# Second product of all six gathered tiles on TensorE, four tokens wide, with a ring of nine shared buffers

## The chip, the cores and the metric

The kernel runs on one core of a Trainium2 chip. The metric is the device time of one launch in microseconds (us), lower is better. TensorE (PE) multiplies, VectorE (DVE) and ScalarE (ACT) work on tiles, GpSimd (POOL) issues the indirect DMAs that gather rows, and SyncE (SP) issues most other DMAs. Each engine takes its instructions in the order in which the program has them.

## The reference

One encoder layer of width 1024 is applied to two groups of tokens, a prompt of 256 and a sample of 1024. Two mixers (a gated recurrence and an attention with low-rank projections) are merged and added to the input. Then a mixture of 16384 small experts follows, and a last norm:

```python
def block(zt):                      # 128 tokens, after the norm with norm_ffn
    ...                             # per token and head (8) the 16 best experts: ids eidx, softmax weights g
    u = jnp.take(u_tab, eidx, axis=0)
    ve = jnp.take(v_tab, eidx, axis=0)
    act = jax.nn.gelu(jnp.einsum('td,thkd->thk', zt, u).astype(jnp.float32), approximate=False) * g
    return jnp.einsum('thk,thkd->td', act.astype(zt.dtype), ve)
...
x = x + _peer(_rmsnorm(x, norm_ffn[l]), ...)
return _rmsnorm(x, norm_final)
```

Each token picks 8 x 16 = 128 experts, so that a tile of 128 tokens needs 128 x 128 rows of 4 KB from each of the two tables. All values are float32.

## The kernel before

Tokens are handled in ten tiles of 128. The experts of six tiles are gathered: the prompt's two (`rP`), the sample's first two (`r0`) and its last two (`r1`). The four tiles between (`rd`) take every expert, with weight zero where it was not picked (`dense`): there TensorE streams both tables, split exactly into two float32r parts, in 2 x 3 x 1024 products of 512 columns.

For a gathered tile `u_steps` makes the first product. For each of its 128 slots one indirect DMA (L933) brings the rows of `peer_u` for all tokens into a buffer `ug`, and one DVE instruction (L935) multiplies them with the normed tokens and sums. Then comes the GELU. The second product has two forms:

- `v_steps` (tiles `rP` and the first of `r0`) works token by token on TensorE. One indirect DMA (L963) brings the 128 picked rows of one token into a buffer `vg`, with picks on the partitions. The token's activations stand in one column of a 32-column block of zeros (`zt`), and a product with it adds the token's result to its row of the PSUM tile `acc` (L970). Tokens of different blocks of 32 use different column groups of the array (`tile_position=(0, g_ * 32)`). Two tokens (VG = 2) are taken together: half row of the first, half row of the second, then the other halves. A float32 product shows as two MATMUL records.
- `v_slots` (the second tile of `r0` and both of `r1`) works slot by slot on DVE: one gather (L989), one multiply-add into the tile `vacc` (L991).

`ug`, `vg` and some scratch share a ring of five buffers of 128 x 1024 float32. The norm vectors `gfin` and `gffn` are loaded once and stay. `experts` takes a step of a tile's first product and a step of the previous tile's second product in turn; the steps of the second product are given high priority.

The order on each engine is written by a planner (`schedule_with_timeline_sim=True`) which runs the program on its own timing model, and puts an instruction in place when its inputs are there in the model; among those that are, high priority goes first. On the chip this order is fixed: PE waits at an instruction whose rows have not landed. `experts(rP)` and `experts(r0 + r1)` are two calls, so a tile's second product runs beside the first product of the next tile of the same call. The last call and `dense` come at the end of the program, and run beside each other.

Of the kernel before, what the change touches and what calls it, by code (L numbers as in the profile page):

```python
# [12 lines left out]
F32 = mybir.dt.float32  # L13
# [11 lines left out]
P = 128  # L25
# [13 lines left out]
VG = 2  # L39
# blocks of the input projection, 128 columns each  # L40
B_Q, B_FF, B_FB, B_I, B_G, B_CQ, B_CKV, B_GLH, B_GLA, B_PE = 0, 4, 8, 12, 16, 20, 23, 25, 33, 41
# columns of the gains
# [8 lines left out]
def encoder(ctx, tc, I, O, dbg=None):  # L51
# [10 lines left out]
    # ---------------------------------------------------------------- constants  # L62
# [21 lines left out]
    # lower bounds: softmax over the two rows, first row  # L84
# [33 lines left out]
    # ---------------------------------------------------------------- helpers  # L118
# [8 lines left out]
    # Operands of the large products come either whole, as (x,) in float32, or split exactly in two  # L127
    # float32r parts, as (high, low).
# [25 lines left out]
    def put(dst, src):  # L154
        # dst: the parts of src
        if len(dst) == 1:
            nc.scalar.copy(dst[0], src)
        else:
            nc.scalar.copy(dst[0], src)  # L159
            nc.vector.tensor_tensor(dst[1], src, dst[0].bitcast(F32), op=OP.subtract)  # L160

    def rsqrt_to(pool, out, src, inv_n, shape, name, vy=None):
        # (src * inv_n + EPS) ** -0.5, one Newton step on exp(-ln/2)
# [9 lines left out]
    def rsqrt_small(pool, out, src, inv_n, shape, name):  # L173
        # the same on VectorE alone, for a few elements: three Newton steps from the exponent's half
# [11 lines left out]
    def norm_T(pool, xs, nk, n, name, bank, fold=False):  # L186
        # xs: [128, n] each, features on partitions; rsqrt of the mean square, on all partitions
# [15 lines left out]
    # ---------------------------------------------------------------- input projection  # L203
    def project(s0, S, ap, wpool, bank, np_, whole):
        """Norm, then blocks of the projection into DRAM; a generator, so that users of the blocks
        can be put between them."""
# [83 lines left out]
    # ---------------------------------------------------------------- HGRN2, one head  # L290
# [3 lines left out]
    def prefixes(hp, f, n, dirs, tg, nb):  # L294
        """From forget gates [P, len(dirs), n] (0 backward, 1 forward): inputs' gates in place of f, prefixes of
        the logarithms inside chunks (backward exclusive, forward inclusive), and the chunks' totals."""
# [26 lines left out]
    def xexp(hp, fb, tot, di, t0, comp, tag):  # L323
        # exp of the prefix, or of what is left to the chunk's end
# [12 lines left out]
    def hgrn_states(s0, S, h, dirs, hp, nb, bank):  # L337
        """States at the chunks' starts."""
# [42 lines left out]
    def hgrn_out(s0, S, h, t0, hp, nb, bank, pre=None):  # L381
        """Outputs of LS tokens: scores inside chunks, level by level, and the states' share."""
# [83 lines left out]
    # ---------------------------------------------------------------- attention  # L466
# [11 lines left out]
    def attn_prep(s0, S, bp, wpool, bank, va, spill):  # L478
        """Latents' norms, then values, and per head keys and queries; these two go to DRAM when spill is set."""
# [8 lines left out]
        for dst, b0, nk, gc in ((ck, 0, 2, G_KVA), (cq, 3, 3, G_QA)):  # L488
# [6 lines left out]
            else:  # L495
                # read into the low part, and split there
# [5 lines left out]
        # keys' rotary part, shared by the heads  # L502
# [13 lines left out]
        # values, token on partitions  # L516
# [41 lines left out]
    def attn_core(s0, nk, q0s, cp, va, keys, queries, bankS, bankT, bankO):  # L558
        """Softmax and values for two heads and QG queries at a time."""
# [95 lines left out]
    # ---------------------------------------------------------------- merge and routing  # L655
    NC_ = 80

    def candidates(cp, vals, top, pos, h0):
        """Best 16 sums of 4 heads. With both lists sorted, the sum of ranks (i, j) has (i + 1)(j + 1) - 1 others
        before it, so that ranks 0 x 16, 1..7 x 8 and 8..15 x 1 hold all of the best; they stay in their order."""  # L660
# [18 lines left out]
    def ranks(cp, pos):  # L679
        # (i, j) of a candidate's place  # L680
# [18 lines left out]
    def merge(s0, t0, G, nd, routes, wpool, rp, bank, wb=3, small=False, tbank=None, tside="left", tctx=None, cut=0, sp=None, mp=None):  # L699
        """Merge, residual and picks of G tokens, of which the first nd tiles' experts are all taken,  # L700
        the others' gathered. Products go by segments of tokens;
        cut: 1 splits the operands of the output's products, 2 those of the branches' too."""
        with ExitStack() as own, ExitStack() as cctx:
# [10 lines left out]
            with ExitStack() as mctx:  # L714
# [39 lines left out]
                def rows(k, x2):  # L754
                    # rows of the residual, and the sum of squares
# [45 lines left out]
            def norm():  # L801
                # what the scores are a factor short of
# [9 lines left out]
            def half(c, hf):  # L812
                # picks of 4 heads: weights and ids
# [72 lines left out]
            def finish_picks(c):  # L886
# [8 lines left out]
                else:  # L895
                    # With an id's halves as 8 (a + 8) + c, and A, C those of a number, 1 - (a - A) ** 2 - (c - C) ** 2
                    # is 1 where they are equal and less than 1 elsewhere; codes are the rows of this product that
                    # belong to the id: 8 a, c, a ** 2 + c ** 2 and 1, small integers all of them.
# [18 lines left out]
            # one half of the dense tiles' picks, and of the first tile's, is done by now  # L917
# [6 lines left out]
    # ---------------------------------------------------------------- experts  # L924
    def u_steps(route):
        tt, gw, ei = route["tt"], route["gw"], route["ei"]
        zs = pe_.tile([P, D], F32, name="zs", tag="zs")
        nc.gpsimd.dma_start(zs, x2d[tt:tt + P])
        nc.vector.scalar_tensor_tensor(out=zs, in0=zs, scalar=route["rt"], in1=gffn, op0=OP.mult, op1=OP.mult)
        dots = pe_.tile([P, P], F32, name="dots", tag="dots", bufs=2)  # L930
        for s in range(P):
            ug = pe_.tile([P, D], F32, name="ug", tag="ring", bufs=5)
            nc.gpsimd.indirect_dma_start(out=ug, out_offset=None, in_=I["peer_u"],  # L933
                                         in_offset=bass.IndirectOffsetOnAxis(ap=ei[:, s:s + 1], axis=0))
            nc.vector.scalar_tensor_tensor(out=ug, in0=ug, scalar=1.0, in1=zs, op0=OP.mult, op1=OP.mult,  # L935
                                           accum_out=dots[:, s:s + 1])
            yield
# [8 lines left out]
    def v_steps(route):  # L946
# [5 lines left out]
        for b in range(4):  # L952
            # a token's activations in its own column, zeros beside it
            zt = zts[0]
            o = (b + 3) % 4 * 8
            nc.vector.memset(ap_of(zt[:, 0, 0, o:o + 1], [[256, 4], [33, 8]]), 0.0)
            nc.vector.tensor_copy(ap_of(zt[:, 0, 0, b * 8:b * 8 + 1], [[256, 4], [33, 8]]), actT[:, :, b * 8:b * 8 + 8])
            for i in range(8):
                vgs = []
                for g in range(4):  # L960
                    t = g * 32 + b * 8 + i
                    vg = pe_.tile([P, D], F32, name="vg", tag="ring", bufs=5)
                    nc.gpsimd.indirect_dma_start(out=vg, out_offset=None, in_=I["peer_v"],  # L963
                                                 in_offset=bass.IndirectOffsetOnAxis(ap=eit[:, t:t + 1], axis=0))
                    vgs.append((g, vg))
                    if len(vgs) == VG:
                        # neighbours in different columns of the array run side by side
                        for n in range(2):
                            for g_, v_ in vgs:
                                nc.tensor.matmul(acc[g_ * 32:(g_ + 1) * 32, n * 512:(n + 1) * 512], zt[:, g_, i],  # L970
                                                 v_[:, n * 512:(n + 1) * 512], start=b == 0 and i == 0,
                                                 stop=b == 3 and i == 7, tile_position=(0, g_ * 32), skip_group_check=True)
                        vgs = []
                    yield
        y = pe_.tile([P, D], F32, name="y", tag="ring", bufs=5)
        x2r = pe_.tile([P, D], F32, name="x2r", tag="ring", bufs=5)
# [5 lines left out]
    def v_slots(route):  # L982
        # the same on VectorE, a slot of every token at a time
        tt, ei, act = route["tt"], route["ei"], route["act"]
        acc = route["acc"].tile([P, D], F32, name="vacc", tag="vacc", bufs=1)
        nc.gpsimd.dma_start(acc, x2d[tt:tt + P])
        for s in range(P):
            vg = pe_.tile([P, D], F32, name="vg", tag="ring", bufs=5)
            nc.gpsimd.indirect_dma_start(out=vg, out_offset=None, in_=I["peer_v"],  # L989
                                         in_offset=bass.IndirectOffsetOnAxis(ap=ei[:, s:s + 1], axis=0))  # L990
            nc.vector.scalar_tensor_tensor(out=acc, in0=vg, scalar=act[:, s:s + 1], in1=acc, op0=OP.mult, op1=OP.add)  # L991
            if s % 2:
                yield
        sq = pe_.tile([P, D], F32, name="sq", tag="ring", bufs=5)
        finish(acc, sq, tt)
        yield

    def finish(y, sq, tt):
# [7 lines left out]
    def weights(routes, gp, bank):  # L1006
        """The picks' weights of a few tiles as a matrix over every expert and token, to DRAM: per token the
        product of its slots' indicators of the id's low half and their weighted indicators of the high half."""
# [44 lines left out]
    def dense(routes, zt, acc, dp, up, bankS, bankV):  # L1053
        """Every expert on a few tiles, those not picked with weight zero; blocks of 128 experts."""
# [36 lines left out]
        for g in range(P // GE):  # L1091
# [3 lines left out]
            second(g)  # L1095
        for t, r in enumerate(routes):
            sq = pe_.tile([P, D], F32, name="sq", tag="ring", bufs=5)
            finish(acc[:, t], sq, r["tt"])

    def experts(routes):  # L1100
        prev = None
        for r in routes + [None]:
            us = u_steps(r) if r else iter(())
            vs = (v_slots if "acc" in prev else v_steps)(prev) if prev else iter(())
# [9 lines left out]
    # ---------------------------------------------------------------- the order of things  # L1114
# [10 lines left out]
    # the prompt up to its routing; the sample's projection comes in as soon as there is room  # L1125
# [31 lines left out]
    gfin = pe_.tile([P, D], F32, name="gfin")  # L1157
    nc.sync.dma_start(gfin, I["norm_final"].partition_broadcast(P))
# [68 lines left out]
    for r in r0[1:] + r1:  # L1227
        r["acc"] = vp
# [81 lines left out]
```

## Time and profile before

| | |
|---|---|
| time, median of 3 runs | 4386.39 us (4372.38 to 4390.8) |
| profiled execution, span from first to last instruction | 4377.9 us |
| PE busy | 4002.2 us, 91% |
| DVE busy | 3375.4 us, 77% |
| ACT busy | 1571.5 us, 36% |
| POOL busy | 1840.3 us, 42% |
| mean granted TensorE clock | 0.959 |
| DMA | 1258.09 MB, mean 287 GB/s |

The profile gives the span of the profiled execution, and no other time of it; the median of the timed runs lies 8.5 us above this span. PE's busy time counts a product from its start to its modelled end, so that neighbours overlap, and a busy PE may still be slowed by what it runs. Idle time is put down to the event that ended it.

### The profile page before, as it was taken

Reading aid. Unit: us, or ns where it says so; the run is one execution under the profiler, and the core shown is the slowest. Engines: PE = TensorE matmul, PEld = TensorE weight load, DVE = VectorE, ACT = ScalarE, POOL = GpSimd, SP = SyncE. Lnnn points to the kernel's source line nnn. Section 1 sums busy time; section 2 is a strip of 40 time slices with the busy share of each in tenths; the row PEclk is TensorE's granted clock in tenths of the full one; section 3 lists DMA queues with packets and bytes.
Section 4 is the critical chain, followed back from the end, with each engine's and each line's share of the span. In section 5 each row is a group of like instructions: output and inputs, shape, how many; then the busy total and the mean of one; then the engine's idle time right before and its main releaser. Section 6 shows DMA issues by size and latency. Waiting matters only on the chain.

```text
span 4377.9 us, 54156 instructions
## 1 busy us (share of the span) xinstructions
PE 4002.2 (91%) x17693; PEld 2741.6 (63%) x17693; DVE 3375.4 (77%) x8088; ACT 1571.5 (36%) x2608; POOL 1840.3 (42%) x1565
## 2 busy tenths in 40 slices
PE   7998999998888999976999949999999999999994
PEld 6787778664434652334654404678888888888883
DVE  4637977466877675388668887869999899999997
ACT  6554474453233213332210117843332233233221
POOL 0000644333444233366445552335555455555554
PEclk9999999999999999988999969999999999999997
DMA  5364999888889877699778776889999999999996
GB/s 166 120 198 132 344 337 332 293 271 282 283 288 308 296 242 265 217 309 351 276 264 277 269 268 224 313 309 341 336 330 341 318 344 343 348 326 354 327 320 230
DMA packets 506731, 1258.09 MB, mean 287 GB/s; under 512 B 49744, under 2 KB 202960, under 8 KB 504400
## 3 DMA queue, kind: packets, MB, share of 16 engines
q0 software_dynamic: 224352, 816.94, 53.3%
q1 hardware_dynamic: 195472, 348.29, 23.5%
q10 hardware_dynamic: 86624, 89.40, 6.0%
q8 instruction: 140, 2.29, 0.2%
q14 instruction: 143, 1.17, 0.1%
HBM read 1159.29 MB, written 95.16 MB: 287 GB/s over the span
## 4 chain that ended last, share of the span: by engine, by line
PE 67%; DMA 10%; DVE 8%; issue 8%; ACT 4%; POOL 3%; POOLq 0%; ACTq 0%; SPq 0%; DVEq 0%
PE pm L140 14%; PE pm L141 14%; PE pm L142 14%; PE pm L138 9%; PE acc L970 7%; DMA ug<-peer_u,ei 5%; DMA vg<-peer_v,eit 3%; PE pm L1043 3%; DVE ug L935 2%; POOL ug L933 2%; PE pm L437 1%; POOL vg L963 1%; PE pm L1024 1%; PE pm L624 1%; PE pm L618 1%
## 5 line engine op out<-in xcount | busy, mean ns | idle before, releaser
L933 POOL DMA_INDIRECT ug<-peer_u,ei x768 | 913.0, 1189 | 915.1 <-DVE ug L935 362.8
L935 DVE SCALAR_TENSOR_TENSOR ug<-ug,zs 128x1024 f32<-128x1024 f32 x768 | 931.6, 1219 | 172.7 <-DMA ug<-peer_u,ei 147.5
L989 POOL DMA_INDIRECT vg<-peer_v,ei x384 | 508.0, 1323 | 454.0 <-DVE vacc L991 280.0
L963 POOL DMA_INDIRECT vg<-peer_v,eit x384 | 404.9, 1055 | 659.1 <-PE acc L970 368.9
L970 PE MATMUL acc<-vg,zt 128*32 128x512 f32 x1536 | 551.5, 643 | 117.6 <-DMA vg<-peer_v,eit 116.0
L991 DVE SCALAR_TENSOR_TENSOR vacc<-vg,act,vacc 128x1024 f32<-128x1024 f32 x384 | 490.9, 1278 | 24.5 <-DMA vg<-peer_v,ei 23.2
L140 PE MATMUL pm<-zth,uh 128*128 128x512 f32 x1024 | 405.2, 396 | 2.4 <-ACT gs L1044 2.0
L142 PE MATMUL pm<-zth,ul 128*128 128x512 f32 x1024 | 405.2, 396 | 0.0
L141 PE MATMUL pm<-ztl,uh 128*128 128x512 f32 x1024 | 404.7, 395 | 0.0
L141 PE MATMUL pm<-vl,ah 128*128 128x512 f32 x1024 | 398.8, 392 | 0.0
L140 PE MATMUL pm<-vh,ah 128*128 128x512 f32 x1024 | 392.4, 393 | 6.1 <-ACT ah L159 3.7
L142 PE MATMUL pm<-vh,al 128*128 128x512 f32 x1024 | 391.6, 392 | 0.0
L970 PEld LDWEIGHTS acc<-vg,zt 128*32 128x32 f32 x1536 | 95.2, 112 | 399.1 <-issue 213.5
L123 ACT CAST vh<-vraw 128x512 fp32r<-128x512 f32 x256 | 157.5, 619 | 445.9 <-DMA vraw<-peer_v 389.6
L138 PE MATMUL pm<-xg,wraw 128*128 128x256 f32 (+1 forms) x1024 | 293.9, 437 | 0.0
L140 PE MATMUL pm<-hh,wh 128*128 128x512 f32 x672 | 268.9, 400 | 5.1 <-ACT gt L255 4.5
L141 PE MATMUL pm<-hl,wh 128*128 128x512 f32 x672 | 267.0, 397 | 0.0
L142 PE MATMUL pm<-hh,wl 128*128 128x512 f32 x672 | 266.3, 396 | 0.0
L123 ACT CAST uh<-uraw 128x1024 fp32r<-128x1024 f32 x128 | 134.6, 1051 | 365.1 <-PE pm L141 344.2
L138 PEld LDWEIGHTS pm<-xg,wraw 128*128 128x128 f32 x1024 | 189.8, 192 | 81.5 <-issue 64.5
L140 PEld LDWEIGHTS pm<-vh,ah 128*128 128x128 f32 x1024 | 193.0, 188 | 50.6 <-ACT ah L159 4.6
L140 PEld LDWEIGHTS pm<-zth,uh 128*128 128x128 f32 x1024 | 192.6, 188 | 49.3 <-ACT gs L1044 2.2
(368 smaller groups left out, 7583.8 us busy)
## 6 DMA issues: line engine op xcount, KB each, us to landing
uraw<-uT SPq DMA_DIRECT2D x128, 512.0 KB, 7.0
vraw<-peer_v SPq DMA_DIRECT2D x256, 256.0 KB, 6.3
wraw<-wi SPq DMA_DIRECT2D x84, 512.0 KB, 4.2
gd<-gs ACTq DMA_DIRECT2D x16, 2048.0 KB, 9.5
g<-gd ACTq DMA_DIRECT2D x32, 1024.0 KB, 18.6
wraw<-wq SPq DMA_DIRECT2D x48, 512.0 KB, 4.0
wraw<-wo SPq DMA_DIRECT2D x24, 512.0 KB, 4.9
ug<-peer_u,ei POOLq DMA_INDIRECT x768, 6.5
```

Of the source, the lines that this page charges most:

```text
L123: nc.scalar.copy(hi, src)
L138: nc.tensor.matmul(out, w[0], x[0], start=start, stop=stop)
L140: nc.tensor.matmul(out, w[0], x[0], start=start, stop=False)
L141: nc.tensor.matmul(out, w[0], x[1], start=False, stop=False)
L142: nc.tensor.matmul(out, w[1], x[0], start=False, stop=stop)
L933: nc.gpsimd.indirect_dma_start(out=ug, out_offset=None, in_=I["peer_u"], in_offset=bass.IndirectOffsetOnAxis(ap=ei[:, s:s + 1], axis=0))
L935: nc.vector.scalar_tensor_tensor(out=ug, in0=ug, scalar=1.0, in1=zs, op0=OP.mult, op1=OP.mult, accum_out=dots[:, s:s + 1])
L963: nc.gpsimd.indirect_dma_start(out=vg, out_offset=None, in_=I["peer_v"], in_offset=bass.IndirectOffsetOnAxis(ap=eit[:, t:t + 1], axis=0))
L970: nc.tensor.matmul(acc[g_ * 32:(g_ + 1) * 32, n * 512:(n + 1) * 512], zt[:, g_, i], v_[:, n * 512:(n + 1) * 512], start=b == 0 and i == 0, ...
L989: nc.gpsimd.indirect_dma_start(out=vg, out_offset=None, in_=I["peer_v"], in_offset=bass.IndirectOffsetOnAxis(ap=ei[:, s:s + 1], axis=0))
L991: nc.vector.scalar_tensor_tensor(out=acc, in0=vg, scalar=act[:, s:s + 1], in1=acc, op0=OP.mult, op1=OP.add)
L1043: nc.tensor.matmul(pm[:, j * P:(j + 1) * P], ol[:, j], oh[:, j], start=True, stop=True)
```

## The change

Every gathered tile's second product now goes through `v_steps`; `v_slots` and its accumulator are gone. In `v_steps` four tokens, one of each block of 32, are taken together: four gathers, then four products on the first half rows and four on the second. `zt` has two halves for alternate blocks of four. The ring has nine buffers, and `gffn` (once per tile, on SP), `gfin` (once per tile and once for `dense`, on SP) are loaded into a buffer of the ring when needed. The scratch of GpSimd's DMA descriptors is 8192 bytes per partition; it was not given before, and the default is 16384.

```diff
-VG = 2
+RING = 9
...
+    def ring(name):
+        return pe_.tile([P, D], F32, name=name, tag="ring", bufs=RING)
...
+        gffn = ring("gffn")
+        nc.sync.dma_start(gffn, I["norm_ffn"].partition_broadcast(P))
...
-        for b in range(4):
+        zt = zts[0]
+        for b in range(8):
+            h = b % 2
+            o = (b + 6) % 8 * 4
+            nc.vector.memset(ap_of(zt[:, h, 0, 0, o:o + 1], [[128, 4], [33, 4]]), 0.0)
+            nc.vector.tensor_copy(ap_of(zt[:, h, 0, 0, b * 4:b * 4 + 1], [[128, 4], [33, 4]]), actT[:, :, b * 4:b * 4 + 4])
+            for i in range(4):
                 vgs = []
                 for g in range(4):
-                    t = g * 32 + b * 8 + i
-                    vg = pe_.tile([P, D], F32, name="vg", tag="ring", bufs=5)
+                    t = g * 32 + b * 4 + i
+                    vg = ring("vg")
                     nc.gpsimd.indirect_dma_start(out=vg, out_offset=None, in_=I["peer_v"],
                                                  in_offset=bass.IndirectOffsetOnAxis(ap=eit[:, t:t + 1], axis=0))
-                    vgs.append((g, vg))
-                    if len(vgs) == VG:
-                        # neighbours in different columns of the array run side by side
+                    vgs.append(vg)
+                    if g == 3:
                         for n in range(2):
-                            for g_, v_ in vgs:
-                                nc.tensor.matmul(acc[g_ * 32:(g_ + 1) * 32, n * 512:(n + 1) * 512], zt[:, g_, i],
+                            for g_, v_ in enumerate(vgs):
+                                nc.tensor.matmul(acc[g_ * 32:(g_ + 1) * 32, n * 512:(n + 1) * 512], zt[:, h, g_, i],
                                                  v_[:, n * 512:(n + 1) * 512], start=b == 0 and i == 0,
-                                                 stop=b == 3 and i == 7, tile_position=(0, g_ * 32), skip_group_check=True)
-                        vgs = []
+                                                 stop=b == 7 and i == 3, tile_position=(0, g_ * 32), skip_group_check=True)
                     yield
...
-    def v_slots(route):
...
+    def final_gain():
+        gfin = ring("gfin")
+        nc.sync.dma_start(gfin, I["norm_final"].partition_broadcast(P))
+        return gfin
...
-            vs = (v_slots if "acc" in prev else v_steps)(prev) if prev else iter(())
+            vs = v_steps(prev) if prev else iter(())
...
-    vp = ctx.enter_context(tc.tile_pool(name="VA", bufs=1, side="right"))
-    for r in r0[1:] + r1:
-        r["acc"] = vp
...
-    nc = _bacc.Bacc("TRN2", target_bir_lowering=False, num_devices=1)
+    nc = _bacc.Bacc("TRN2", target_bir_lowering=False, num_devices=1, dynamic_dma_scratch_size=8192)
```

## Rows read from the trace of the kernel before

**Rows 1.** Windows by stage: us, each engine's busy us (instructions), clock, DMA share, GB/s.

```profile
766.00:1467.00 701.00, 633.21 (x2656) 358.65 (x2654) 496.14 (x1247) 259.53 (x417) 269.35 (x260) 0.97 0.86 289
1467.00:1840.00 373.00, 362.62 (x1556) 163.64 (x1555) 196.58 (x868) 100.93 (x223) 127.50 (x132) 0.99 0.75 248
2104.00:2700.00 596.00, 515.79 (x1972) 252.82 (x1969) 442.06 (x1804) 123.06 (x192) 282.08 (x254) 0.92 0.79 269
2700.00:2885.00 185.00, 171.53 (x1014) 113.55 (x1013) 141.50 (x278) 157.70 (x219) 44.33 (x43) 0.96 0.74 274
2885.00:4318.00 1433.00, 1426.00 (x6144) 1155.82 (x6144) 1309.56 (x1747) 427.61 (x646) 764.41 (x588) 1.00 0.94 333
4318.00:4378.00 60.00, 0.13 (x1) 0.00 (x0) 41.35 (x86) 5.75 (x10) 23.88 (x22) 0.52 0.57 204
```

**Rows 2.** Waits of PE from 2885 to 4318 us, the longest of four: us, times, longest.

```profile
PE pm L140 <- ACT ah L159: 3.7, 2, 3.0
```

**Rows 3.** Waits of PE for gathered rows, by stage: 766:1467, 1467:1840, 2104:2700.

```profile
PE acc L970 <- DMA vg<-peer_v,eit: 41.0, 21, 5.0
...
PE acc L970 <- DMA vg<-peer_v,eit: 10.3, 6, 2.6
...
PE acc L970 <- DMA vg<-peer_v,eit: 64.7, 29, 5.5
```

**Rows 4.** The page's costliest groups: busy us, mean ns, idle before and its releaser.

```profile
L970 PE MATMUL acc<-vg,zt 128*32 128x512 f32 x1536 | 551.5, 643 | 117.6 <-DMA vg<-peer_v,eit 116.0
L991 DVE SCALAR_TENSOR_TENSOR vacc<-vg,act,vacc 128x1024 f32<-128x1024 f32 x384 | 490.9, 1278 | 24.5 <-DMA vg<-peer_v,ei 23.2
L963 POOL DMA_INDIRECT vg<-peer_v,eit x384 | 404.9, 1055 | 659.1 <-PE acc L970 368.9
```

**Rows 5.** Timeline of PE, 856 to 863 us: start, us, what.

```profile
856.38 0.39 PE L141 MATMUL pm<-hl,wh 128*128 128x512 f32 x1
856.70 1.90 PE L970 MATMUL acc<-vg,zt 128*32 128x512 f32 x6
858.53 0.50 PE L142 MATMUL pm<-hh,wl 128*128 128x512 f32 x1
858.87 0.40 PE L140 MATMUL pm<-hh,wh 128*128 128x512 f32 x1
...
861.20 0.39 PE L141 MATMUL pm<-hl,wh 128*128 128x512 f32 x1
861.51 1.04 PE L970 MATMUL acc<-vg,zt 128*32 128x512 f32 x2
862.49 0.50 PE L142 MATMUL pm<-hh,wl 128*128 128x512 f32 x1
862.83 0.39 PE L140 MATMUL pm<-hh,wh 128*128 128x512 f32 x1
```

**Rows 6.** Timeline of PE: L970 in eight records; in first and last group of all.

```profile
785.15 1.04 PE L970 MATMUL acc<-vg,zt 128*32 128x512 f32 x2
...
1477.89 1.91 PE L970 MATMUL acc<-vg,zt 128*32 128x512 f32 x8
...
2697.41 1.91 PE L970 MATMUL acc<-vg,zt 128*32 128x512 f32 x6
```

**Rows 7.** Timeline of POOL, 1005 to 1016 us: gathers of one pair, and the next.

```profile
1005.01 0.94 POOL L963 DMA_INDIRECT vg<-peer_v,eit  x1 [3.85 <-DVE ug L935]
...
1016.14 0.94 POOL L963 DMA_INDIRECT vg<-peer_v,eit  x1 [5.22 <-PE acc L970]
1017.38 0.94 POOL L933 DMA_INDIRECT ug<-peer_u,ei  x1 [0.30 <-issue]
```

**Rows 8.** Timeline of all engines from 4318 us: the tail.

```profile
4318.16 0.69 DVE L1086 TENSOR_TENSOR acc<-pm,acc 128x512 f32<-128x512 f32 x1 [0.44 <-PE pm L142]
...
4349.21 2.61 DVE L991 SCALAR_TENSOR_TENSOR vacc<-vg,act,vacc 128x1024 f32<-128x1024 f32 x2 [0.26 <-DMA vg<-peer_v,ei]
...
4353.22 1.06 ACT L1000 ACTIVATE sq<-acc 128x1024 f32<-128x1024 f32 x1 [0.22 <-DVE finv L177]
```

**Rows 9.** Source view of L963: time from issue to landing of its gathers.

```profile
DMA to landing us min/median/max: 4.0/5.7/11.5
```

More of the change, by code (lines that the diff above doesn't have):

```diff
@@ L931, in u_steps @@
         for s in range(P):
-            ug = pe_.tile([P, D], F32, name="ug", tag="ring", bufs=5)
+            ug = ring("ug")
             nc.gpsimd.indirect_dma_start(out=ug, out_offset=None, in_=I["peer_u"],
@@ L951, in v_steps @@
         nc.vector.tensor_copy(actT.rearrange("p g i -> p (g i)"), acc[:, 0:P])
-        for b in range(4):
[L954 to L958, printed above, removed]
+        zt = zts[0]
[5 more added lines that the diff above has]
+            for i in range(4):
@@ L974, in v_steps @@
                     yield
-        y = pe_.tile([P, D], F32, name="y", tag="ring", bufs=5)
-        x2r = pe_.tile([P, D], F32, name="x2r", tag="ring", bufs=5)
+        y = ring("y")
+        x2r = ring("x2r")
         nc.gpsimd.dma_start(x2r, x2d[tt:tt + P])
@@ L980, in v_steps, with finish @@
         yield
-    def v_slots(route):
[L984 to L998, printed above, removed]
+    def final_gain():
+        gfin = ring("gfin")
+        nc.sync.dma_start(gfin, I["norm_final"].partition_broadcast(P))
+        return gfin
+    def finish(y, sq, tt, gfin=None):
+        gfin = final_gain() if gfin is None else gfin
         ss = pe_.tile([P, 1], F32, name="fss", tag="fss")
@@ L1095, in dense @@
             second(g)
+        gfin = final_gain()
         for t, r in enumerate(routes):
-            sq = pe_.tile([P, D], F32, name="sq", tag="ring", bufs=5)
-            finish(acc[:, t], sq, r["tt"])
+            finish(acc[:, t], ring("sq"), r["tt"], gfin)
     def experts(routes):
@@ L1156, in encoder @@
     pe_ = ctx.enter_context(tc.tile_pool(name="peer", bufs=1, side="right"))
-    gfin = pe_.tile([P, D], F32, name="gfin")
-    nc.sync.dma_start(gfin, I["norm_final"].partition_broadcast(P))
-    gffn = pe_.tile([P, D], F32, name="gffn")
-    nc.sync.dma_start(gffn, I["norm_ffn"].partition_broadcast(P))
-    zts.append(pe_.tile([P, 4, 8, 32], F32, name="zt0"))
+    zts.append(pe_.tile([P, 2, 4, 4, 32], F32, name="zt0"))
     for z_ in zts:
```

## The prediction

> **What bounds the kernel now.** I read the windows by stage first. In the last long stage, 2885 to 4318 us, PE is busy 1426.0 of 1433 us at full clock, and has 6144 records, the products of `dense` alone: 1433 / 6144 = 0.233 us each [rows 1]. The waits of PE there are four short ones, the longest 3.7 us in total [rows 2]. So this stage is bound by PE. DVE, with 1309.6 us, is nearly full beside it, and so are the DMA engines (share 0.94), but PE hardly waits for either. What DVE does for the second product, 384 instructions of 1278 ns or 491 us [rows 4], lies almost wholly in this stage and beside PE. Before it PE is bound less strictly: 90, 97 and 87% busy in the three stages in which `v_steps` runs [rows 1]. Its waits for gathered rows there are 41.0, 10.3 and 64.7 us, 116 in all [rows 3, 4]. After the last product of `dense` 60 us remain [rows 1]: DVE still has the rest of the last `v_slots` to do, and the first square for `dense` starts at 4353.22 [rows 8].
>
> So the change takes work from an engine that hides it, and gives it to the one that doesn't. What it costs is set by how PE runs these products, and that the timeline shows.
>
> **What a product of L970 costs.** [Rows 5] has two groups among float32r products, whose starts are 0.23 us apart. Six records: from 856.38 to 858.87 are 2.49 us; less two ordinary products (0.46) the group costs PE 2.03. Two records: from 861.20 to 862.83 are 1.63, less 0.46 is 1.17. The two records are one half row of one token, alone: the first token's rows had landed in the planner's model, the second's not. The six are the other three products of the pair: first half of token two beside second half of token one, then the last one. Eight records together take 1.91 us to their end, as long as six (1.90) [rows 5, 6]: the pair's four products in two column groups, two abreast. So a pair that stays together costs 2.03, a pair that is split 3.20. The program's order is kept among these products; no group has the first token's two halves ahead of the second token. Counted in the timeline, between the first and the last of these groups [rows 6], 53 of 64 pairs of the first tile are split, 36 of the second, 23 of the third (shares 0.83, 0.56 and 0.36). The first tile runs beside a first product and a busy PE, so that each `vg` is followed by a `ug`; the second is gathered alone.
>
> **With four tokens.** If nothing is split, a group of four has eight products in four column groups: each group passes two, as in a pair, so 2.03 if four run abreast. If each of the three boundaries is split, three lone products go ahead (3 x 1.17), and five remain, which take two passes: 2.03 again. So a group costs 2.03 + 3 x s x 1.17 with a share s of boundaries split, and a tile has 32 groups. No row shows four abreast. The bounds are that four run like two (2.03), and that only two run at once: five products then need three turns of two passes, 2.03 + 0.86 (0.86 being two passes: the 0.98 us from 861.51 to 862.49 less the 0.12 by which it ends early), and eight need four turns, 2.03 + 1.72. I take the lower one, since two abreast lose nothing in [rows 6]. The Trainium skill, TensorE: Matmul & The Clock Gate, section Measured speedup vs the span model, gives 2.38 times for three column tiles and 3.07 for four row tiles. By 3.07 an unsplit group would be about 2.24 us plus the switch, an estimate that adds some 20 us to the stage; the trace has no four to compare.
>
> **The sum.**
> - *`dense` stage.* The second tile of `r0` and the first of `r1` run beside a first product and a busy PE, so s = 0.83: 32 x (2.03 + 2.91) = 158 us each. The last one runs alone, s = 0.56: 32 x (2.03 + 1.97) = 128. Sum +444. Bounds: +195 (s = 0) to +613 (s = 1 and two abreast: 96 x 6.40). About 20 of it can go ahead of the stage, since the first product of `r1` may start in 2700 to 2885, where PE is 93% busy with short products [rows 1] (0 to 40): -20.
> - *Three earlier tiles.* Before: 3 x 64 x 2.03 + 112 x 1.17 = 521 us. After, with the same three shares, 158 + 128 + 105 = 391. Of the tiles' savings (34, 44 and 52) the first two count in full, PE being 90 and 97% busy, the third by half: -104. Bounds: 0, and 521 - 195 = 326.
> - *Waits for rows.* With five buffers a pair's next gathers start when the pair is done: 11.1 us from one pair's `vg` to the next in [rows 7], two steps of the alternation, of which some 6 are landing (median 5.7 [rows 9]). With nine, eight gathers share one landing: 8 x 1.24 us of issue (1016.14 to 1017.38) and 6 us of landing make 16 for four steps, 4 us a step in place of 5.5. PE then waits less for rows: half of 116, -58 (0 to -116). The DMA share, 0.75 to 0.86 in these stages [rows 1], has room for it.
> - *New waits.* In the `dense` stage each group now stands in PE's fixed order, and all of `dense` is queued behind it. Before, a late row held up DVE alone. I take a third of the 116 us for three tiles, 40 (0 to 150), as landings in a stage with DMA share 0.94 are no quicker than in the earlier ones.
> - *The tail.* With no `vacc` left, the squares for `dense` can follow its last sum, which ends at 4318.85, in place of 4353.22: -34 (0 to -34). The rest, four norms and the output, stays.
> - *At nothing.* DVE's relief of 491 us: PE is idle for 7 us in the stage, all told [rows 1]. `zt`'s doubled memsets and copies, and the added residual sums, go to the time that DVE gains. The 13 loads of norm vectors (0.5 MB each, against 1258 MB): but SP waits in order for a free buffer, and `dense`'s loads are queued behind. PE has two `uraw` ahead of it, 24 products each; if that cover fails, 13 x 5.7 = 74 us. Half the descriptor scratch: if it held fewer than nine gathers, the gain of 58 would go, no more; no row shows it filled.
>
> 4377.9 - 104 - 58 + 444 - 20 + 40 - 34 = 4646 us of span. The profiled execution's span is 8.5 us below the median of the runs; I add these: **4655 us**, 6% slower.
>
> **The rivals.**
> - *Groups stay whole* (15%). If in the planner's model four rows land close together, or wait for PE together, nothing is split, as in 41 of 64 pairs of the third tile. Then `dense` gets 195 - 10, the early tiles save 326, of which 0.8 count (261), and 58 of waits: 4378 - 261 - 58 + 185 + 40 - 34 = 4250, 4258 with the 8.5: faster by 3%. It decides where s falls below about 0.2. Against it: nine buffers let gathers out one at a time, 2.5 us from one `vg` to the next while `ug` alternate, and PE has work in between. The Trainium skill, TensorEngine Tiling (Array Packing), section Theoretical Speedup, gives up to four times for 32 columns, which is this case; the trace shows two at most.
> - *Half split* (13%), s = 0.4 throughout: a group is 3.43, three tiles 330. 4378 - 0.8 x 191 - 58 + 330 - 15 + 40 - 34 = 4488, so 4497.
> - *Two abreast only* (12%): 0.86 more per group, 83 us in `dense` and 66 early: about 4805.
> - *PE is paced by the gathers* (8%). Three tiles at the third tile's wait, 64.7 each, make 194 in place of 40: 4810. The stage's DMA share of 0.94 speaks for it; that it becomes longer by PE's work, with the same bytes, against.
> - That the change is one of order alone, and PE's added work fits into waits, is excluded: the stage has 7 us of idle PE.
>
> The forecast has 50%, with 4500 to 4800 as its own range. The range for 8 times in 10 is 4330 to 4880: it leaves out most of the first rival and what lies above two abreast with stalls. A measurement tells 0.5% (22 us) from no change. Faster by more: 0.19 (the first rival and a little of the second); within: 0.04; slower: 0.77.
>
> **What would show it.** PE's records in the stage of `dense` rise from 6144 by 1536, and the stage lengthens by about 440 us with PE full. The timeline has L970 in groups of 2, 2, 2 and 10 records there; groups of 16 mean the first rival. Ten records should end in 1.9 us; 2.8 mean two abreast. DVE falls to some 60% of the stage. L970's waits for `vg` in it stay near 40 us; more means that gathers pace it. The stages before 2885 get shorter by 160 us, and the squares for `dense` begin right behind its last sum. A stage of `dense` longer by less than 250 us would prove the forecast wrong, and so would early stages shorter by more than 300.

## The result, and the profile after

After the change the kernel takes 4804.59 us in the median (4798.01 to 4808.31), before it 4382.52 in the runs beside them: the ratio is 1.0965 [1.0943, 1.0986]. The direction was right and the time lies within the range, but the kernel lost 425 us of span (4377.9 to 4802.9), where the sum said 268.

By stage, in the windows of the kernel after (columns as in [rows 1]), the whole stretch ahead of `dense`, two stretches of it in which PE is short of work, the stage of `dense`, and the tail:

```profile
0.00:2881.00 2881.00, 2517.81 (x11653) 1583.57 (x11653) 2014.96 (x6294) 1131.94 (x1947) 1086.21 (x975) 0.93 0.77 271
...
1702.00:2106.00 404.00, 280.91 (x1232) 114.59 (x1233) 305.77 (x659) 137.54 (x316) 262.56 (x224) 0.82 0.89 311
...
2456.00:2704.00 248.00, 185.54 (x800) 113.71 (x799) 221.59 (x1199) 105.47 (x161) 0.95 (x2) 0.85 0.20 71
...
2881.00:4788.00 1907.00, 1905.30 (x7580) 1196.91 (x7580) 922.93 (x1456) 430.91 (x653) 624.48 (x587) 1.00 0.73 252
4788.00:4803.00 15.00, 0.00 (x0) 0.00 (x0) 8.51 (x34) 1.15 (x2) 1.59 (x3) 0.61 0.30 124
```

The same window ahead of `dense` of the kernel before:

```profile
0.00:2885.00 2885.00, 2576.11 (x11549) 1585.78 (x11549) 2024.47 (x6255) 1138.11 (x1953) 1052.00 (x957) 0.95 0.78 267
```

So `dense` begins 4 us earlier, its stage grows from 1433 to 1907 us (+474), and the tail shrinks from 60 to 15 (-45): -4 + 474 - 45 = 425. The stage is full of PE, 1905.30 of 1907 us. Ahead of it PE's busy time fell by 58.3 us, and its idle time rose by 54.3 (2885 - 2576.11 = 308.9 before, 2881 - 2517.81 = 363.2 after).

The product of the change on the page after (columns as in [rows 4]):

```profile
L976 PE MATMUL acc<-vg,zt 128*32 128x512 f32 x3072 | 893.8, 610 | 25.4 <-DMA vg<-peer_v,eit 25.4
```

The instructions doubled, and the wait for rows fell from 116.0 us [rows 4] to 25.4. How PE runs them, in the timeline of PE after, within the stage of `dense` (columns as in [rows 5]):

```profile
3599.87 0.40 PE L142 MATMUL pm<-zth,ul 128*128 128x512 f32 x1
3600.20 1.05 PE L976 MATMUL acc<-vg,zt 128*32 128x512 f32 x2
3601.17 0.50 PE L140 MATMUL pm<-zth,uh 128*128 128x512 f32 x1
3601.51 0.39 PE L141 MATMUL pm<-ztl,uh 128*128 128x512 f32 x1
...
3604.76 0.40 PE L140 MATMUL pm<-zth,uh 128*128 128x512 f32 x1
3605.09 1.90 PE L976 MATMUL acc<-vg,zt 128*32 128x512 f32 x10
3606.93 0.50 PE L141 MATMUL pm<-ztl,uh 128*128 128x512 f32 x1
3607.26 0.39 PE L142 MATMUL pm<-zth,ul 128*128 128x512 f32 x1
...
3608.99 1.04 PE L976 MATMUL acc<-vg,zt 128*32 128x512 f32 x2
```

Lone products of two records, then the other five of the group in ten: the split group of four, 2, 2, 2 and 10 records, as forecast (the rows show the last lone product of one group, its ten, and the first lone one of the next group). A lone product costs 3601.51 - 3599.87 - 2 x 0.233 = 1.17 us, the ten 3607.26 - 3604.76 - 0.466 = 2.03. Counted in the timeline, the last three tiles have 89, 92 and 91 lone products in their 32 groups each, 272 of 288 possible (s = 0.94); the first three have 82, 36 and 64, and 16 pieces of two products besides.

Ahead of `dense`, the waits of PE from 766 to 2881 us in the kernel after (us in total, times, longest):

```profile
PE pm L138 <- ACT pn L606: 67.8, 22, 10.9
PE pm L892 <- DVE ids L843: 54.6, 2, 49.9
PE pm L912 <- DVE gw L827: 43.4, 4, 18.4
PE acc L976 <- DMA vg<-peer_v,eit: 25.4, 12, 3.9
PE pm L871 <- ACT qT L867: 14.4, 17, 4.1
```

and two of the kernel before, from 766 to 2885, which shows none for `ids` and none for `qT`:

```profile
PE pm L138 <- ACT pn L606: 38.2, 19, 5.2
...
PE pm L912 <- DVE gw L827: 7.3, 1, 7.3
```

Where the rows cost 91 us less, 135 us (30 + 55 + 36 + 14) came up in waits for attention (`pn`, the softmax), the picks (`ids`, `qT`) and their weights (`gw`). The longest one, in PE's timeline and in DVE's work (as groups) during it:

```profile
1822.88 0.48 PE L892 MATMUL pm<-ident,ids 128*128 128x128 f32 x1 [49.90 <-DVE ids L843]
```

```profile
L940 DVE SCALAR_TENSOR_TENSOR ug<-ug,zs 128x1024 f32<-128x1024 f32 x36 | 43.3, 1216 | 1.6 <-DMA ug<-peer_u,ei 1.4
L840 DVE TENSOR_TENSOR scr<-scr 128x128 bf16<-128x128 bf16 (+2 forms) x10 | 3.2, 317 | 0.0
```

In 50 us, 1773 to 1823, DVE spends 43.3 on 36 sums of the next tile's first product (the first of `r0`), and the short steps that lead to `ids` (the second row is the largest of them) stand between those sums. In the kernel before, the last `ids` of this stage are done before these sums begin; in the kernel after, the sums begin first. The last `ids` before, the first sum before, the first sum after:

```profile
1694.06 0.28 PE L892 MATMUL pm<-ident,ids 128*128 128x128 f32 x1
...
1843.10 1.22 DVE L935 SCALAR_TENSOR_TENSOR ug<-ug,zs 128x1024 f32<-128x1024 f32 x1
```

```profile
1709.90 1.21 DVE L940 SCALAR_TENSOR_TENSOR ug<-ug,zs 128x1024 f32<-128x1024 f32 x1
```

The waits for `gw` and `qT` have another cause. They lie between 2456 and 2704 us, where no sum of a first product and no product of L976 runs: the third tile's last product ends at 2455.67, and in the kernel before at 2699.32 [rows 6]. DVE is 89% busy there with the next picks and with `dense`'s weights, and the DMA share is 0.20. The third tile's last product, and GpSimd's next gather:

```profile
2453.77 1.90 PE L976 MATMUL acc<-vg,zt 128*32 128x512 f32 x10
```

```profile
2703.59 0.98 POOL L938 DMA_INDIRECT ug<-peer_u,ei  x1 [220.05 <-DVE ei L845]
```

GpSimd stands 220 us at the first gather of the first `r1` tile, whose ids (`ei`) are not there yet. The gathers for the second product of the second `r0` tile, whose `ids` PE had at 1823, come behind it in GpSimd's order, and so four fifths of that product (410 of 512 records) fall into the stage of `dense`. No run tried another order of the gathers.

### The profile page after: what moved, and what is told of

Its sections match the earlier page's. It is cut to its first block, busy times and chain, and to the rows that moved or that the text cites. A ratio compares the mean times of both kernels' runs of the same rounds, so it can differ in the third digit from the quotient of the medians.

```text
span 4802.9 us, 56915 instructions
## 1 busy us (share of the span) xinstructions
PE 4423.1 (92%) x19232; PEld 2780.5 (58%) x19232; DVE 2946.4 (61%) x7782; ACT 1564.0 (33%) x2602; POOL 1712.3 (36%) x1565
## 4 chain that ended last, share of the span: by engine, by line
PE 72%; issue 10%; DVE 8%; DMA 5%; ACT 3%; POOL 1%; SPq 0%; ACTq 0%; POOLq 0%; DVEq 0%
PE acc L976 16%; PE pm L140 12%; PE pm L141 12%; PE pm L142 12%; PE pm L138 10%; PE pm L1038 3%; DVE ug L940 2%; DMA ug<-peer_u,ei 2%; PE pm L1019 1%; PE pm L624 1%; PE pm L618 1%; PE pm L437 1%; PE pm L871 1%; DMA vg<-peer_v,eit 1%; POOL ug L938 1%
## 5 line engine op out<-in xcount | busy, mean ns | idle before, releaser
L938 POOL DMA_INDIRECT ug<-peer_u,ei x768 | 873.8, 1138 | 1077.5 <-DVE ug L940 371.5
L969 POOL DMA_INDIRECT vg<-peer_v,eit x768 | 824.2, 1073 | 1150.5 <-PE acc L976 500.0
L976 PE MATMUL acc<-vg,zt 128*32 128x512 f32 x3072 | 893.8, 610 | 25.4 <-DMA vg<-peer_v,eit 25.4
L1081 DVE TENSOR_TENSOR acc<-pm,acc 128x512 f32<-128x512 f32 x256 | 170.9, 687 | 386.4 <-PE pm L142 385.7
L142 PE MATMUL pm<-vh,al 128*128 128x512 f32 x1024 | 404.6, 397 | 0.0
L124 DVE TENSOR_TENSOR ul<-uraw,uh 128x1024 fp32r<-128x1024 f32 x128 | 156.7, 1224 | 389.5 <-ACT uh L123 363.3
L140 PE MATMUL pm<-vh,ah 128*128 128x512 f32 x1024 | 373.3, 401 | 0.3 <-DVE acc L1081 0.3
L976 PEld LDWEIGHTS acc<-vg,zt 128*32 128x32 f32 x3072 | 142.2, 108 | 377.1 <-issue 320.8
L141 PEld LDWEIGHTS pm<-vl,ah 128*128 128x128 f32 x1024 | 192.2, 188 | 91.1 <-issue 44.4
```

The lines of the kernel that those rows point to most:

```text
L124: (eng or nc.vector).tensor_tensor(lo, src, hi.bitcast(F32), op=OP.subtract)
L140: nc.tensor.matmul(out, w[0], x[0], start=start, stop=False)
L141: nc.tensor.matmul(out, w[0], x[1], start=False, stop=False)
L142: nc.tensor.matmul(out, w[1], x[0], start=False, stop=stop)
L1081: nc.vector.tensor_tensor(acc[:, t, ns], pm, acc[:, t, ns], op=OP.add)
```

## The experiments

The reasons to be tested: that the order of the products costs the stage, and why the early savings did not come. All ratios are to the kernel before.

**whole.** The products of a group are issued in the order three, two, one, zero, so the first one needs the row that is gathered last.

```diff
-                            for g_, v_ in enumerate(vgs):
+                            for g_, v_ in reversed(list(enumerate(vgs))):
```

> The kernel after, with the products of a group of four issued in the order 3, 2, 1, 0, so that the first one needs the row that lands last and no product goes ahead alone. Theory A (the stage of dense grew by PE's time for the added products, and over half of that is the lone ones): L976 in groups of 16 records, each 2.03 us of PE among float32r products; three lone products per group less, so 3 tiles x 32 x 2.85 x 1.17 = 320 us off the stage of dense, 1907 to about 1590; total 4480 (4440 to 4530). Rival B (PE is paced by the rows: a group that waits for its last row holds all of dense behind it): the stage stays over 1800, with waits of PE for vg of 200 us or more; total over 4680. Rival C (four products do not run abreast): 16 records take 3.7 us, total about 4650.

Measured: 4420.13 us, 1.0087 [1.0059, 1.0116]. A group of the timeline of PE, and the stage of `dense`:

```profile
3392.55 0.40 PE L140 MATMUL pm<-zth,uh 128*128 128x512 f32 x1
3392.88 1.92 PE L976 MATMUL acc<-vg,zt 128*32 128x512 f32 x16
3394.73 0.50 PE L141 MATMUL pm<-ztl,uh 128*128 128x512 f32 x1
```

```profile
2775.00:4404.00 1629.00, 1615.38 (x7583) 1182.29 (x7584) 922.94 (x1451) 434.93 (x653) 628.13 (x588) 1.00 0.82 295
```

All 192 groups are of 16 records. PE waits 1.9 us for `vg` in the stage, and a group ends in 1.92 us, so rivals B and C fall. The stage is 1629 - 1433 = 196 us longer than before, and 96 groups at 2.03 are 195: theory A holds, and the prediction's price of a whole group with it. The stage is longer than the expectation of this run had it (1590), and the time lower than its 4440 to 4530, since `dense` also begins 106 us sooner than in the changed kernel. With the same work and bytes as there, the order alone is worth 385 us: 278 in the stage, 106 ahead of it.

**late_dve.** The changed kernel, with the last three tiles' second product on DVE as before (`v_slots` and its accumulator come back), and the ring of nine kept.

```diff
...
-            vs = v_steps(prev) if prev else iter(())
+            vs = (v_slots if "acc" in prev else v_steps)(prev) if prev else iter(())
```

> The kernel after, with the second product of the last three gathered tiles back on DVE (slot by slot), everything else as after: ring of nine, norm vectors on demand, half scratch, first three tiles four wide. Theory A: the stage of dense is back at 1433 us with 6144 records and starts where it does after (about 2880), since what the earlier tiles save does not arrive; total 4340 to 4385, the lower part if the larger ring lets the last DVE tile end before dense does. Rival D (ring and four-wide products do shorten the early stages by the 160 us that were forecast, and something in the late form takes it back): 4250 or less.

Measured: 4609.64 us, 1.0515 [1.0497, 1.0533], a clear miss. The stage of `dense` takes 1693 us with the 6144 products that took 1433 before. Its first part, up to 3900, and the rest, then its longest waits of PE:

```profile
2905.00:3900.00 995.00, 827.73 (x3225) 636.63 (x3226) 935.70 (x1238) 229.96 (x343) 669.37 (x520) 0.92 0.98 368
3900.00:4598.00 698.00, 683.01 (x2918) 552.04 (x2918) 398.93 (x530) 206.77 (x310) 74.49 (x59) 0.99 0.47 156
```

```profile
PE pm L141 <- DVE vl L124: 92.2, 37, 6.2
PE pm L140 <- DVE acc L1095: 22.9, 17, 4.7
```

Up to 3900 DVE is 94% busy and DMA at 0.98; PE passes 3225 products in the time of 995 / 0.233 = 4270. Afterwards DVE is 57% busy, and a product takes 698 / 2918 = 0.239 us again. With nine buffers the gathers run ahead, DVE's multiply-adds with them, and `vl`, which DVE makes for `dense`, comes late.

**late_dve_whole.** Both edits together, those of whole and of late_dve.

> As late_dve, and the first three tiles' groups kept whole by the order 3, 2, 1, 0. PE's work for these tiles falls from about 500 us to 195. Theory A2 (the stages before dense are set by a chain through attention, merge, routing and picks, with DVE in it, and not by PE's amount of work): dense starts within 30 us of late_dve, total within 30 us. Rival D2 (PE's amount of work sets them): dense starts about 200 us earlier.

Measured: 4486.9 us, 1.0231 [1.0205, 1.0257]. `dense` begins at 2772 in place of 2905, and its stage stays at 1701. So the order is worth 133 us in the three early tiles of this kernel, more than the 30 and less than the 200 that the two theories gave. The early tiles' time did become shorter here, so it was not all hidden.

**late_dve_five.** late_dve, with only five of the nine buffers in use once a tile with `acc` is running (two tags, of four and five).

```diff
...
+        turn[0] += 1
+        if turn[1] or turn[0] % RING >= 4:
+            return pe_.tile([P, D], F32, name=name, tag="ringb", bufs=RING - 4)
+        return pe_.tile([P, D], F32, name=name, tag="ringa", bufs=4)
...
+            turn[1] = bool(prev and "acc" in prev)
```

> late_dve, but from the first product of the first r1 tile on (all that runs beside dense) only five of the nine buffers are used in turn. Theory E (with nine buffers the gathers and their DVE work run ahead of dense, fill DVE and the DMA engines, and PE waits for split operands, 92 us on vl alone; five buffers throttle them): the stage of dense falls from 1693 to 1433-1460 us with no wait for vl over 10 us, and starts about 2900 as before; total 4380 to 4420. Rival G (not the ring, but other parts of the change, such as the norm vectors' loads that wait on SP ahead of dense's loads, stretch that stage): it stays over 1600, total over 4560.

Measured: 4363.07 us, 0.995 [0.9931, 0.9969]. The stage of `dense`, and the longest wait of PE in it:

```profile
2886.00:4321.00 1435.00, 1425.10 (x6144) 1153.19 (x6143) 1306.21 (x1743) 429.69 (x645) 761.85 (x585) 1.00 0.94 332
```

```profile
PE pm L140 <- ACT ah L159: 8.1, 1, 8.1
```

The stage is back at 1435 us, and the wait for `vl` is 0.4 in all. Theory E holds: the 258 us of late_dve come from the nine buffers beside `dense`. The time is lower than the 4380 to 4420 that it gave, as `dense` begins at 2886.

**late_dve_whole_five.** All three edits.

> late_dve_whole with the same five buffers beside dense. It is late_dve_five with the first three tiles' groups of four kept whole. If theory E holds and the earlier start of dense that whole groups gave (2772 against 2905 us) stays, the total is 2772 + 1440 + 60, about 4270 (4250 to 4310), faster than the kernel before by 2 to 3%. By rival G it is over 4420.

Measured: 4255.0 us, 0.9701 [0.9685, 0.9718], faster than both kernels, and within its expectation. Its stage of `dense` is the old one, begun 118 us sooner:

```profile
2767.00:4200.00 1433.00, 1424.88 (x6142) 1153.34 (x6143) 1307.21 (x1744) 428.73 (x646) 748.62 (x585) 1.00 0.94 333
```

The groups are not all whole here, though the order of the products is that of whole. Counted in the timeline, 50 of the 96 show as 16 records; in late_dve_whole, with one tag, all 96 do. Why the order does less with two tags stays open.

**pairs_whole.** The kernel before, its pairs issued second token first.

```diff
-                            for g_, v_ in vgs:
+                            for g_, v_ in reversed(vgs):
```

> The kernel before, with the two products of a pair issued in the order 1, 0, so that no pair is split; nothing else changed. PE has 112 lone products less, 131 us, all of it before the stage of dense. Theory A2: total 4350 to 4390, since the chain before dense isn't PE's. Rival D2: 4280 or less.

Measured: 4349.47 us, 0.9921 [0.9906, 0.9936]. The 112 lone products (131 us at 1.17) are gone, but `dense` begins only 32 us sooner, at 2853. The time is close to what theory A2 gave and far from rival D2. PE now waits longer for rows, 173.7 us in place of 116.0 [rows 4]:

```profile
PE acc L970 <- DMA vg<-peer_v,eit: 173.7, 63, 9.6
```

**first_cut.** The changed kernel, with the first product of the first `r0` tile on DVE over 32 of 1024 columns; the rest of that product is left out.

```diff
+            w = slice(0, 32) if tt == SEQS[1][0] else slice(0, D)
-            nc.vector.scalar_tensor_tensor(out=ug, in0=ug, scalar=1.0, in1=zs, op0=OP.mult, op1=OP.mult,
+            nc.vector.scalar_tensor_tensor(out=ug[:, w], in0=ug[:, w], scalar=1.0, in1=zs[:, w], op0=OP.mult, op1=OP.mult,
```

> The kernel after, with the first product of the first r0 tile on DVE over 32 of 1024 columns (the rest of that product is left out). Theory F (what the early tiles save is lost since DVE is full with that tile's first products while PE waits for DVE's maxima and ids: 55 us for ids and 64 us for pn between 1385 and 2106 us): the wait for ids goes below 10 us and the one for pn below 40, dense starts 60 to 110 us earlier than 2881; total 4690 to 4745. Rival H (the chain there is ScalarE's and PE's own): waits and total stay within 20 us of after (4803).

Measured: 4728.11 us, 1.0788 [1.0759, 1.0817]. The waits of PE over the whole span, the three longest, and the window from 1385 to 2106:

```profile
PE pm L912 <- DVE gw L827: 50.2, 4, 27.4
PE acc L977 <- DMA vg<-peer_v,eit: 28.0, 19, 5.7
PE pm L138 <- ACT pn L606: 17.8, 18, 3.0
```

```profile
1385.00:2106.00 721.00, 646.41 (x3170) 353.90 (x3171) 407.59 (x1585) 225.77 (x481) 336.00 (x335) 0.95 0.90 319
```

The wait at L892, where `ids` come in, is down to 4.5 us and that for `pn` by 50 us; PE passes 3170 products in this window, where the changed kernel passes 2746 (1514 + 1232). `dense` begins at 2791, 90 us sooner. So these sums are what `pn` and `ids` wait for (theory F). They are not what `gw` and `qT` wait for: these two waits stay, at 50.2 and 15.4 us. The kernel before has the same sums and was not run with the cut: the 90 us are their price in the changed kernel, not the difference between the two.

**whole_r5.** whole with a ring of five.

```diff
-RING = 9
+RING = 5
```

> whole with a ring of five in place of nine. By theory F slower gathers crowd DVE less: PE's waits for ids, gw, pn and qT (204 us in whole) fall by 60 us or more, its waits for vg rise (29 to 100 us or more); dense starts within 40 us of 2775. The stage of dense is 1617 us of PE work if the rows keep up (three steps of 4.5 us for each group's landing are 1540 us for the three tiles, about the same): 1620 to 1720. Total 4400 to 4520. Rival I (the larger ring is what brought the earlier start): dense starts at 2850 or later.

Measured: 4928.73 us, 1.1242 [1.1223, 1.1261], again a miss. The waits for `ids` and `pn` leave the head of the list, as theory F wants, and `dense` begins at 2741, 34 us sooner than in whole, so rival I falls. But four of the five buffers hold one group, and the rows pace everything else: PE waits 494.9 us for `vg`. Most of it comes behind `dense`, in the waits of PE from 4458 us:

```profile
PE acc L976 <- DMA vg<-peer_v,eit: 321.3, 35, 16.5
```

The first products of the last two tiles take 5.7 us a slot in place of 5.3 and 4.9 before, so their second products come late, and the last one is still being gathered when `dense` has ended. In these runs four tokens at a time need the deeper ring.

**scratch.** The kernel before, with half the descriptor scratch.

```diff
-    nc = _bacc.Bacc("TRN2", target_bir_lowering=False, num_devices=1)
+    nc = _bacc.Bacc("TRN2", target_bir_lowering=False, num_devices=1, dynamic_dma_scratch_size=8192)
```

> The kernel before with one part of the change alone: half the descriptor scratch (8192 bytes per partition). The prediction cost this at nothing. If that holds, the time stays within 0.3% of 4383 us, PE's waits for vg stay near 116 us, and the median landing of the second product's gathers stays near 5.7 us. Rival J: the scratch limits how many gathers are out at once; then the waits of GpSimd grow, the waits for vg rise by 30 us or more, and the time by 20 to 60 us.

Measured: 4375.44 us, 0.9991 [0.9976, 1.0006]. The wait for `vg` is 101.1 us, no more than before. The time from issue to landing is not in this trace. With five buffers the smaller scratch costs nothing; with nine it was not taken away by itself.

**best_seven.** late_dve_whole_five with seven buffers ahead of `dense` (tags of two and five).

```diff
-RING = 9
+RING = 7
...
-        if turn[1] or turn[0] % RING >= 4:
-            return pe_.tile([P, D], F32, name=name, tag="ringb", bufs=RING - 4)
-        return pe_.tile([P, D], F32, name=name, tag="ringa", bufs=4)
+        if turn[1] or turn[0] % RING >= 2:
+            return pe_.tile([P, D], F32, name=name, tag="ringb", bufs=RING - 2)
+        return pe_.tile([P, D], F32, name=name, tag="ringa", bufs=2)
```

> The version with the late tiles on DVE, whole groups and five buffers beside dense, but with seven buffers instead of nine ahead of dense. Theory F (the faster gathers of nine buffers give DVE more sums at the moments at which attention and the picks need it, and PE waits for ids, pn and gw): these waits fall, and dense starts before 2767 us, at 2720 to 2760; the time is 4205 to 4250 us. Rival K (PE needs nine buffers in order not to wait for rows): the waits for vg rise by 40 us or more over those of nine, dense starts after 2790, and the time is 4280 to 4340 us.

Measured: 4269.49 us, 0.9757 [0.9732, 0.9783], slightly slower than nine. The longest waits of PE with seven, and the same with nine:

```profile
PE acc L982 <- DMA vg<-peer_v,eit: 144.6, 45, 15.4
PE pm L138 <- ACT pn L606: 43.0, 17, 6.5
...
PE pm L912 <- DVE gw L827: 8.0, 1, 8.0
```

```profile
PE pm L138 <- ACT pn L606: 63.0, 23, 10.1
PE pm L892 <- DVE ids L843: 46.5, 1, 46.5
PE pm L912 <- DVE gw L827: 43.4, 4, 18.4
PE acc L982 <- DMA vg<-peer_v,eit: 33.1, 12, 4.6
```

Both theories are half right: `pn`, `ids` and `gw` give back some 100 us, as F says, and the rows take 112 more, as K says. `dense` begins at 2774, 7 us later than with nine, which is between the two forecasts. The wait for `ids` is gone here, and the first `r0` tile's sums begin at 1769, after the last `ids` of that stage (made at 1642). The depth of the ring is not the only difference: with seven, 95 of the 96 groups of the first three tiles are whole, and with nine 50. The 43 pieces that go ahead there are some 50 us of PE's work at 1.17, which the seven buffers save, and still they gain nothing.

## Why the prediction was right, and where it failed

| term of the sum | forecast, us | measured, us |
|---|---|---|
| early tiles, PE's own work | -104 | -94 (521 to 198 x 1.17 + 96 x 2.03 = 427) |
| waits for rows | -58 | -91 (116.0 to 25.4) |
| all else ahead of `dense` | none | +147 (the balance) |
| group work of the last three tiles | +444 | +513 (272 x 1.17 + 96 x 2.03) |
| of it done ahead of the stage | -20 | 34 moved, no gain |
| new waits in the stage | +40 | -5 |
| tail | -34 | -45 |

The 34 us are those 102 of the last three tiles' 1536 records that lie ahead of 2881 (513 x 102 / 1536). So the stage grew by 513 - 34 - 5 = 474, and ahead of it -94 - 91 + 34 + 147 = -4. The 198 are the 182 lone products and the 16 pieces of two, which are priced like a lone one: the two such pieces in the stage of `dense` take 1.30 and 1.31 us from the start of the product before to that of the one behind, a lone product 1.30 in the median.

- **The number.** The time lies in the range, but 5 us above the 4500 to 4800 that the forecast named as its own, and at what two rivals gave: two abreast (4805) and pacing by the gathers (4810). The records rule out both, as said below, so that their figures fit by chance.
- **The step that failed** is the pair of early terms, -104 and -58. Both savings came, 185 us together, and the early tiles' products ended 244 us sooner, but `dense` began only 4 us sooner. The prediction took 90 and 97% of PE busy as a sign that PE sets the pace there. But PE stood in a chain with DVE and ACT. The sums of the third tile moved ahead of the picks that DVE has to make beside them (they begin at 1710, the last `ids` come at 1823; before, 1843 and 1694), and PE waited for `ids` and `pn`. Behind that, from 2456 to 2704, the experts' products had run out, and PE waited for `gw` and `qT`, with the next tiles' picks and weights as the only work left. The balance of 147 is 145 us of more idle PE beside the rows' own (54 + 91) and 2 of busy time; the mean clock was 0.93 in place of 0.95, and what that costs was not separated. first_cut shows the first part, the waits for `ids` and `pn`, and best_seven agrees. The second part is read from the trace and was not tried by a run. pairs_whole shows that 131 us of PE work saved there are worth 32 even with a ring of five (58 of them went into longer waits for rows).
- **Dense stage.** The mechanism was right, and the price of a lone product (1.17) and of a rest (2.03) were read to the hundredth. Mis-sized was the share: 0.94 for all three tiles in place of 0.83, 0.83 and 0.56, which is 69 us. I took 0.56 for the last tile because it is gathered alone; it has 91 lone products all the same. What the planner's model saw there can't be read from the trace.
- **New waits.** 40 us were allowed, none came: no wait for `vg` from 2881 on, so the gathers do not pace PE there. The size was wrong on the safe side, and with the 34 us moved it makes up most of the 69.
- **Four abreast.** Ten records end in 1.90 us and sixteen in 1.92 us, eight of the pair in 1.91 [rows 6]: the rival with two abreast falls. The ends are modelled, but the starts around them say the same: 2.17 us with ten, 2.18 with sixteen, 2.15 with six [rows 5]. The prediction's estimate of some 20 us more leaves out the switch that it names: its group of 2.03 is two turns of 0.86 and 0.31 of switching, so 2.24 and 0.31 would have been 50 us over 96 groups. Neither shows. The Trainium skill, TensorEngine Tiling (Array Packing), section Theoretical Speedup, gives up to four times for 32 columns; these rows agree, with 16 records in four column groups in the time of eight in two. The Trainium skill, TensorE: Matmul & The Clock Gate, section Measured speedup vs the span model, has 2.38 times for three column tiles, less than three; no such loss shows here.
- **Groups stay whole.** As a rival this was priced at 4258; made to happen, in whole, it took 4420. The stage was priced at +195 and measured +196; its early savings, priced at 319, came to 110 (`dense` from 2885 to 2775), by the step above.
- **DVE** is 48% busy in the stage (922.93 of 1907 us), not 60: the forecast divided what is left by the old length of the stage.
- **The tail** gained 11 us more, since of the norms only the last tile's remains behind its last sum (it ends at 4788.48, and the last square starts at 4788.65):

```profile
4788.65 1.06 ACT L995 ACTIVATE sq<-acc 128x1024 f32<-128x1024 f32 x1 [0.77 <-DVE finv L177]
```

- **At nothing.** The scratch cost nothing, in a run of its own with five buffers. The norm vectors and `zt` head no wait of PE's lists; they were not run by themselves.
- **Not foreseen**, and no part of the changed kernel: with DVE's form kept beside it, the ring of nine would have cost the stage of `dense` 258 us (late_dve against late_dve_five).

## What to carry to other kernels

Where the order on an engine is written ahead from a timing model, issue first the instruction whose input arrives last: the group then stays together, and here this is worth 385 us. Look in the timeline whether it does: with the buffers in two tags half of the groups broke all the same. In this kernel a stage in which PE was 90 to 97% busy did not give its savings, because DVE stood in the chain; ask what the engine that feeds it will be doing when the work is pulled forward, and what is left to do when that work has run out. A deeper ring is a throttle opened, so its depth belongs to a stage: here nine buffers where PE waited for rows, five where DVE and DMA were full.

## What the runs showed of the hardware that was not expected

- Float32 products of 32 columns in four column groups run abreast without a loss against two: sixteen records end in 1.92 us, eight in two column groups in 1.91 [rows 6].
- A lone product among full-width ones costs PE 1.17 us, and a group of eight products 2.03: whole has 96 groups in the stage of `dense`, and the stage is 196 us longer.
- The mean granted clock was lower where PE waited: 0.92 in late_dve from 2905 to 3900 us with PE 83% busy, and 0.82 in the changed kernel from 1702 to 2106 with PE 70% busy. Around the wait of 49.9 us there, from 1747 to 1828, it was 0.50, the lower of the two levels (1.2 of 2.4 GHz), with PE busy for 12 of 81 us. It was 1.00 in the stages with PE full.
